# Modulation products beside the projections: issued in groups of eight and of four row blocks instead of two

## The chip, the cores and the metric

The kernel runs on one core of one Trainium2 chip. The core has TensorE (matrix products, 128 x 128 cells), VectorE, ScalarE, GpSimd and SyncE, which here only issues transfers; each works through its own list of instructions in order, and semaphores hold an instruction back until what it needs is there. The metric is the device time of one execution in microseconds (us), lower is better. Before the change it is 2209.9 us, the median of three runs (2208.8 to 2213.77).

## The reference

One step of a two-layer trunk over 1024 latent and 256 context tokens of width 1024, in 32-bit floats. Cut to the parts that matter here:

```python
def _pre(x, cond, p):
    mod = (jax.nn.silu(cond) @ p['w_ada'] + p['b_ada'])[:, None, :]
    shift, scale, gate = jnp.split(mod, 3, axis=-1)
    h = rms_norm(x, p['norm_g']) * (1 + scale) + shift
    parts = jnp.split(h @ p['w_in'], idx, axis=-1)
    return parts, gate

def _post(x, o_ret, o_gqa, o_mla, z_gate, g_res, w_out):
    y = jnp.concatenate([o_ret, o_gqa, o_mla], axis=-1) * jax.nn.silu(z_gate)
    return x + g_res * (y @ w_out)
```

`cond` is one vector for the latent tokens and one for the context tokens, so the modulation is a product of two rows of 1024 with a matrix `w_ada` of 1024 x 3072 in each layer: shift, scale and gate are its thirds. Between `_pre` and `_post` stand a retention, a grouped-query attention and a latent attention over the parts of `h @ w_in`.

## The kernel before

The tokens are ten tiles of 128. A projection block (`blk`, line 441) takes 256 columns of `w_in` (288 in one block) and makes, tile by tile, `act^T W` in one accumulator bank of PSUM (`project`, line 248). Activations and weights are each split into a high and a low part so that three fast products, lines 255 to 257, add up to full precision: 3 x 8 = 24 matmuls for a tile. The activations of the first layer are made while its first block runs (`phase_a`, line 373: transposes on TensorE, line 384, scale and shift on ScalarE and VectorE, lines 391 and 393, splits on ScalarE and VectorE, lines 401 and 402). The weights come as granules of two row blocks, are split by GpSimd (lines 191 and 192) and go into rings; three staging buffers, loaded at line 225, feed the splits, and a load into one of them waits until the split that read it last is done.

The modulation is `ada` (line 285). `cond` holds both conditioning vectors, 32 columns wide with two in use, so a product of one row block of 128 rows needs only 32 of the array's 128 columns. Four products can therefore stand side by side in four column tiles of the array (`tile_position`, line 329): row block k goes to column tile k % 4, and the tiles' sums are added afterwards. For each group of 256 columns, eight row blocks are multiplied, a load (line 316, 256 KB) bringing two of them at a time:

```python
for g in range(4):
    raw = raws.pop(0)
    for kk in range(2):
        k = 2 * g + kk
        ...
    load()
    yield
```

The `yield` is how this work is spread: `ada` is a generator, and each step of it runs after a tile of a projection block. The first two thirds of layer 0's modulation run ahead of everything. Its gate (columns 2048 to 3071, 64 products into tag "o", `gate_ada`, line 1463) runs beside the first projection block of layer 0, two steps after each tile. All of layer 1's modulation (96 products into tag "acc", `rest_of_ada`, line 1467) runs beside blocks two to seven of layer 0, one step after each tile and none in the fourth. Weights of the gate have a ring of eleven tiles, those of layer 1 a ring of three, of which `load()` fills at most two ahead. When a group of 256 columns is done, its sum is copied out (line 336) and, steps later, transposed (line 295).

The tag "acc" has five banks: four are free for projections while the modulation holds one. The tag "o" has a bank of its own.

What sets the order: the program is written in order, and a scheduler then places each engine's instructions by their dependences and priorities into the fixed list that the engine works through. SyncE issues nearly all transfers, also those of `w_in` and the stores of results, from one such list, so a transfer that waits holds back those after it.

Of the kernel before, what the change touches and what calls it, by code (L numbers as in the profile page):

```python
# [84 lines left out]
def hybrid_trunk(tc, I, O):  # L85
# [9 lines left out]
    # ------------------------------------------------------------------ DRAM scratch  # L95
# [12 lines left out]
    # ------------------------------------------------------------------ persistent pools  # L108
# [11 lines left out]
    def yh(t):  # L120
        """The columns of the attention heads, [P, GQA or MLA, head, 64]: head i of both side by side."""
        return yx[t][:, Y_H:].rearrange("p (i s c) -> p s i c", s=2, c=64)
# [21 lines left out]
    def newton(ss, n, c, bufs=4):  # L144
        """rsqrt(ss * c + EPS) for [P, n]."""
        x = sm.tile([P, 8], F32, name="nwx", tag="nwx")[:, :n]
        y = sm.tile([P, 8], F32, name="nwy", tag="nwy")[:, :n]
        u = sm.tile([P, 8], F32, name="nwu", tag="nwu")[:, :n]
        V.tensor_scalar(x, ss, c, EPS, op0=ALU.mult, op1=ALU.add)
        V.tensor_scalar(u.bitcast(I32), x.bitcast(I32), 1, None, op0=ALU.arith_shift_right)  # L150
        V.tensor_scalar(y.bitcast(I32), u.bitcast(I32), -1.0, float(0x5F3759DF), op0=ALU.mult, op1=ALU.add)
        V.tensor_scalar(x, x, -0.5, None, op0=ALU.mult)
        for _ in range(3):
            if n == 1:
                V.scalar_tensor_tensor(u, y, y, x, op0=ALU.mult, op1=ALU.mult)
            else:
                V.tensor_tensor(u, y, y, op=ALU.mult)
                V.tensor_tensor(u, u, x, op=ALU.mult)
            V.scalar_tensor_tensor(y, u, 1.5, y, op0=ALU.add, op1=ALU.mult)
        return y  # L160

    def rsq(ss, n, c):
        """rsqrt(ss * c + EPS) for [P, n]: exp(-ln / 2) and a Newton step."""
        return rsq_end(rsq_start(ss, n, c))
# [39 lines left out]
    class Weights:  # L204
        """Column blocks of [1024, *] matrices, split, as rings of K-granules of two row blocks."""
# [42 lines left out]
    def project(act, gran, n):  # L248
        """acc[tok, n] = act^T W, all three products of the split operands."""
        ps = bank("acc")[:, :n]  # L250
        ah, al = act
        for k in range(KC):
            wh, wl = gran[k // 2]
            wh, wl = wh[:, k % 2, :n], wl[:, k % 2, :n]
            T.matmul(ps, ah[:, k, :], wh, start=(k == 0), stop=False)  # L255
            T.matmul(ps, ah[:, k, :], wl, start=False, stop=False)  # L256
            T.matmul(ps, al[:, k, :], wh, start=False, stop=(k == KC - 1))  # L257
        return ps

    # ------------------------------------------------------------------ conditioning  # L260
# [12 lines left out]
    def ada_rows():  # L273
        """b_ada and norm_g of every layer with the columns on the partitions."""
        rows = wp.tile([P, 128], F32, name="brow", tag="msb", bufs=1)
        for l in range(DEPTH):
            dma(rows[32 * l:32 * l + 24, :], I["b_ada"][l].rearrange("(k p) -> k p", p=P))
            dma(rows[32 * l + 24:32 * l + 32, :], I["norm_g"][l].rearrange("(k p) -> k p", p=P))
        ps = bank("m")
        T.transpose(ps[:, :32 * DEPTH], rows[0:32 * DEPTH, :], ident[0:32 * DEPTH, 0:32 * DEPTH])  # L280
        for l in range(DEPTH):
            V.tensor_copy(biasT[l], ps[:, 32 * l:32 * l + 24])
            V.tensor_copy(normT[l], ps[:, 32 * l + 24:32 * l + 32])

    def ada(l, ns, pool, bufs, tag, wait=1, lag=1, done=None):
        """modT[l][:, 2n..2n+1, :] for the 256-column groups ns of the modulation; both
        conditionings at once, the row blocks of w_ada in four column tiles of the array."""
# [34 lines left out]
        for x, n in enumerate(ns):  # L322
            ps = bank(tag)[:, :256]
            for g in range(4):
                raw = raws.pop(0)
                for kk in range(2):
                    k = 2 * g + kk
                    j = k % 4
                    T.matmul(ps[32 * j:32 * j + 32, :], cond[:, k, :],
                             raw[:, kk, :], start=(k < 4), stop=(k >= 4), tile_position=(0, 32 * j))  # L330
                load()
# [20 lines left out]
    # ------------------------------------------------------------------ phase A: modulated norm, transposed and split  # L352
# [16 lines left out]
    def norm_x(t, junk):  # L369
        """x / rms(x) in place."""  # L370
        scale_x(t, rstd_x(t, junk))
# [32 lines left out]
    # ------------------------------------------------------------------ rope on natural [P, heads, dim]  # L404
    def rope(dst, src, cos, sin, h, dim, pa, eng=None):
        """dst = src * cos + rotate(src) * sin (signs are in sin)."""
# [13 lines left out]
    # ------------------------------------------------------------------ phase B: input projection  # L420
# [17 lines left out]
    def phase_b(l, p1, acts, ws, first, first_side, first_done, att):  # L438
# [63 lines left out]
        # ---- MLA query up-projection weights  # L502
# [16 lines left out]
        def cq_rest(t):  # L519
            """What is left of the tiles before t: transposes, up-projection, transposes, a tile per stage."""  # L520
# [38 lines left out]
        def cq_queries(t, qo):  # L559
            """The rotary queries of tile t transposed, to memory."""  # L560
# [42 lines left out]
        def headnorm(ps):  # L603
            """Per-head rms norm of four heads of 64."""
# [10 lines left out]
        def weighted_rope(g, nm):  # L615
            """rope tables with the norm weights in them: rope(x * g) = x * gc + rotate(x) * gs."""
# [38 lines left out]
        def gqa_transposed(t, o):  # L655
            """The queries of both attentions of tile t transposed in their place, the keys to memory."""
# [11 lines left out]
        def z_blk(c, post):  # L668
            """Gates of 256 columns with the columns on the partitions: the retention's, or those of two heads of each attention."""
# [64 lines left out]
    # ------------------------------------------------------------------ retention  # L734
# [12 lines left out]
    def decays(tmp):  # L747
        """log sigmoid of the decay logits (log1p as an atanh series), and the decays of every layer."""
# [16 lines left out]
        # q fwd, q bwd, k fwd, k bwd (the key scale 1/8 is in the last two)  # L765
# [7 lines left out]
    def retention(l, rt):  # L773
        if True:
# [20 lines left out]
            def increments(t, kv):  # L795
# [11 lines left out]
                # forward state after chunk t  # L807
# [4 lines left out]
                # backward increments, scanned below  # L812
# [87 lines left out]
    def cache_keys(l, pool, bufs):  # L900
        """The cached keys of both attentions, transposed."""
# [19 lines left out]
    def latents(l, lt):  # L921
        """Keys and values of the MLA heads from the compressed ones, in blocks of four chunks."""
# [56 lines left out]
    def decay_masks(l, pool, bufs):  # L979
        """The two directions' decays between the tokens of a chunk, with the key scale 1/8."""  # L980
# [23 lines left out]
    # ------------------------------------------------------------------ attention  # L1004
    class Attention:
# [3 lines left out]
        def prepare(self):  # L1009
            """Keys, values and queries of the first head, on the right side."""  # L1010
# [11 lines left out]
    def attention(l, att):  # L1022
        """Twelve heads over (latent pair x 4, context pair), software-pipelined by key banks:
        scores, softmax, transposes, values each some steps behind the one before."""
# [5 lines left out]
        # What keys and values are made of: pairs of a load into a staging tile and of its use  # L1030
# [9 lines left out]
        def k_items(i, src, K, split):  # L1040
            """[hi; lo] of 64 rows of transposed keys."""
# [57 lines left out]
        def kr_items():  # L1099
            """[hi; lo; hi; lo] of the transposed rotary keys, for rotary queries [hi; hi; lo; lo]."""  # L1100
# [16 lines left out]
        def q_piece(p):  # L1117
            """Queries of two token tiles, [hi; hi] and [lo; lo], and the rotary ones [hi; hi; lo; lo]."""
# [32 lines left out]
        def items():  # L1151
            """Keys and values of all heads, in the order of use; a function holds the uses after it back while it is false."""
# [14 lines left out]
        def step(force=False):  # L1167
            """Load an item, and use the one loaded some steps before."""
# [29 lines left out]
        # ---- the pipeline  # L1198
# [88 lines left out]
        def head_cols(p):  # L1287
            """Head p.i of both attentions, transposed, of two token tiles."""
# [4 lines left out]
        def y_job(p):  # L1293
            """The outputs of a pair of both heads by the sums of their softmaxes."""
# [11 lines left out]
        def advance(jobs):  # L1306
            """One pipeline step; jobs: the score job of this step, or none at the end."""
# [23 lines left out]
        # ---- pairs of token tiles: those of the GQA heads first, then in turn with those of the MLA heads  # L1331
# [63 lines left out]
    # ------------------------------------------------------------------ phase D: gate, output projection, residual  # L1395
# [5 lines left out]
    def phase_d(l, p1, acts, ws, after):  # L1401
        with tc.tile_pool(name=f"pg{l}", reuse_waits="tile", bufs=1, side="right") as pg, tc.tile_pool(name=f"pd{l}", reuse_waits="tile", bufs=1, side="right") as pd:
# [10 lines left out]
            def gated(t):  # L1413
                """The gated outputs of tile t, split; x comes back in their place."""
# [40 lines left out]
    # ------------------------------------------------------------------ the trunk  # L1455
# [7 lines left out]
    def gate_ada(pool, bufs):  # L1463
        yield from ada(0, range(8, 12), pool, bufs, "o", WG)
        ada_gate(0)

    def rest_of_ada(pool, bufs):
        yield from ada(1, range(12), pool, bufs, "acc", WR)
# [71 lines left out]
    for l in range(DEPTH):  # L1540
# [8 lines left out]
        def scale_late(t):  # L1549
            """1 / rms of tile t, and x / rms of the tile before it, whose copy is in s_x by then."""  # L1550
# [97 lines left out]
```

## Time and profile before

| | |
|---|---|
| median of three runs | 2209.9 us (2208.8 to 2213.77) |
| profiled execution: span from first to last instruction | 2203.2 us |
| distance of the median of the runs to that span | 6.7 us |
| TensorE busy | 2115.8 us, 96% |
| VectorE, ScalarE, GpSimd busy | 1555.0, 1183.4, 893.2 us |
| mean granted clock of TensorE | 0.990 of 2.4 GHz |

The profile is of one execution, and the other runs have no span of their own, so the 6.7 us stand for all that lies around the span. A matmul's row shows a start and a duration; matmuls are pipelined, so the step from one start to the next, not the duration, is what one costs in a stream. A row that ends in xN stands for N neighbouring instructions alike. A 32-bit product of `ada` leaves two records (two passes), and four of them make a pair. Text in brackets at a row's end is idle time of the engine before it and what ended it.

### The profile page before, as it was taken

What the parts mean: (1) busy time and instruction counts of PE and PEld (TensorE: products, weight loads), DVE (VectorE), ACT (ScalarE), POOL (GpSimd) and SP (SyncE); (2) the same over time, 40 slices, a digit from 0 to 9 for tenths busy, and PEclk for the clock granted to TensorE, in tenths of its full rate; (3) what the DMA queues carried; (4) which work ended last, traced back from release to release, by engine and by line L of the source; (5) the groups of instructions that cost most, each with busy time, mean ns of one, the idle gap of its engine ahead of it and who ended that gap; (6) DMA issues with size and microseconds to landing.
All of it is one profiled execution on the core that took longest, in us unless ns stands there. A gap on an engine that the chain in (4) does not pass through costs nothing. (4 is left out here: it accounts for less than half of the span.)

```text
span 2203.2 us, 42098 instructions
## 1 busy us (share of the span) xinstructions
PE 2115.8 (96%) x14928; PEld 1881.0 (85%) x14928; DVE 1555.0 (71%) x3987; ACT 1183.4 (54%) x3151; POOL 893.2 (41%) x1322
## 2 busy tenths in 40 slices
PE   7999999998999999999999999999899999999998
PEld 3789887877888888888999999888788888888898
DVE  4625474567898999998265357556699899999834
ACT  4503223233888888885244133313388888888623
POOL 2332232303756555432533314321375655443274
PEclk9999999999999999999999999999999999999999
DMA  9442435523100000014333212452310000001432
GB/s 322 126 137 60 122 93 167 159 64 100 32 25 20 22 21 16 5 51 124 97 133 108 59 51 58 130 158 75 95 42 23 22 23 22 11 9 32 135 101 96
DMA packets 196954, 173.15 MB, mean 79 GB/s; under 512 B 34968, under 2 KB 179208, under 8 KB 196744
## 3 DMA queue, kind: packets, MB, share of 16 engines
q1 hardware_dynamic: 195304, 165.21, 25.5%
q10 hardware_dynamic: 1440, 5.24, 0.6%
q8 instruction: 119, 1.95, 0.4%
q14 instruction: 91, 0.75, 0.1%
HBM read 124.64 MB, written 45.76 MB: 77 GB/s over the span
## 5 line engine op out<-in xcount | busy, mean ns | idle before, releaser
L257 PE MATMUL acc<-wh,al 128*128 128x256 f32 (+1 forms) x1760 | 500.0, 284 | 7.5 <-DVE al L402 7.4
L255 PE MATMUL acc<-wh,ah 128*128 128x256 f32 (+1 forms) x1760 | 505.3, 287 | 0.2
L256 PE MATMUL acc<-wl,ah 128*128 128x256 f32 (+1 forms) x1760 | 502.2, 285 | 0.0
L1219 DVE TENSOR_REDUCE nm<-acc 128x1 f32<-128x512 f32 (+1 forms) x624 | 412.2, 666 | 41.8 <-PE acc L1213 25.8
L1256 DVE TENSOR_TENSOR pT<-tp,pT 128x512 fp32r<-128x512 f32 (+1 forms) x624 | 413.2, 664 | 32.6 <-ACT pT L1255 27.4
L1255 ACT CAST pT<-tp 128x512 fp32r<-128x512 f32 (+1 forms) x624 | 356.1, 572 | 145.5 <-PE tp L1251 139.2
L1233 ACT ACTIVATE pn<-acc,nm 128x512 f32<-128x512 f32 (+1 forms) x624 | 421.4, 681 | 21.7 <-DVE nm L1224 19.6
L1251 PE MATMUL tp<-ident,pn 128*128 128x128 f32 x2400 | 424.7, 274 | 4.5 <-DVE pT L1256 3.0
L255 PEld LDWEIGHTS acc<-wh,ah 128*128 128x128 f32 x1760 | 334.3, 190 | 23.3 <-issue 9.1
L257 PEld LDWEIGHTS acc<-wh,al 128*128 128x128 f32 x1760 | 331.4, 188 | 11.1 <-DVE al L402 11.0
L256 PEld LDWEIGHTS acc<-wl,ah 128*128 128x128 f32 x1760 | 333.4, 189 | 1.2 <-issue 0.8
L1267 PE MATMUL o<-pT,V 128*128 128x256 f32 x1200 | 325.7, 293 | 0.8 <-DVE yx L1280 0.7
L1251 PEld LDWEIGHTS tp<-ident,pn 128*128 128x128 f32 x2400 | 288.5, 141 | 35.9 <-PE tp L1251 5.8
L1268 PE MATMUL o<-pT,V 128*128 128x256 f32 x1200 | 314.6, 284 | 0.0
L1267 PEld LDWEIGHTS o<-pT,V 128*128 128x128 f32 x1200 | 226.4, 189 | 19.8 <-DVE yx L1280 5.7
L1268 PEld LDWEIGHTS o<-pT,V 128*128 128x128 f32 x1200 | 226.7, 189 | 16.3
L191 POOL TENSOR_SCALAR wh<-raw 128x512 fp32r<-128x512 f32 (+2 forms) x144 | 84.8, 598 | 383.6 <-PE acc L257 150.1
L192 POOL TENSOR_TENSOR wl<-raw,wh 128x512 fp32r<-128x512 f32 (+2 forms) x144 | 166.5, 1167 | 4.9
L680 PE MATMUL acc<-ah,wh 128*128 128x512 f32 (+1 forms) x384 | 142.7, 372 | 0.0
L1210 PE MATMUL acc<-K,Qm 128*128 128x512 f32 (+1 forms) x312 | 140.5, 450 | 1.0
L681 PE MATMUL acc<-ah,wl 128*128 128x512 f32 (+1 forms) x384 | 139.4, 363 | 0.0
L682 PE MATMUL acc<-al,wh 128*128 128x512 f32 (+1 forms) x384 | 139.3, 363 | 0.0
(276 smaller groups left out, 3913.3 us busy)
## 6 DMA issues: line engine op xcount, KB each, us to landing
raw<-in_w_ada_dram SPq DMA_DIRECT2D x96, 256.0 KB, 3.5
raw<-in_w_in_dram SPq DMA_DIRECT2D x56, 256.0 KB, 3.7
s_gT<-eo SPq DMA_DIRECT2D x80, 128.0 KB, 2.5
kv<-s_rkv SPq DMA_DIRECT2D x40, 256.0 KB, 2.9
gt<-s_gT SPq DMA_DIRECT2D x20, 512.0 KB, 4.9
yx<-in_x_sample_dram SPq DMA_DIRECT2D x16, 512.0 KB, 8.6
raw<-in_w_in_dram SPq DMA_DIRECT2D x56, 128.0 KB, 2.2
raw<-in_w_out_dram SPq DMA_DIRECT2D x48, 128.0 KB, 3.0
```

Source lines behind the costliest of these rows:

```text
L192: G.tensor_tensor(wl, raw, wh.bitcast(F32), op=ALU.subtract)
L255: T.matmul(ps, ah[:, k, :], wh, start=(k == 0), stop=False)
L256: T.matmul(ps, ah[:, k, :], wl, start=False, stop=False)
L257: T.matmul(ps, al[:, k, :], wh, start=False, stop=(k == KC - 1))
L680: T.matmul(ps, wh, ah[:, k, :], start=(k == 0), stop=False)
L1219: V.tensor_reduce(nm[:, b:b + 1], ps, axis=AX.X, op=ALU.max, negate=True)
L1233: A.activation(pn, ps, AF.Exp, bias=p.ng[i], accum_out=p.su[:, i, b:b + 1])
L1251: T.transpose(pt[:, c * 128:(c + 1) * 128], pn[:, c * 128:(c + 1) * 128], ident)
L1255: A.copy(ph, p3)
L1256: V.tensor_tensor(pl, p3, ph.bitcast(F32), op=ALU.subtract)
L1267: T.matmul(p.po, vc, p.gran[b][:, 0, c, :], start=(ch == 0), stop=False)
L1268: T.matmul(p.po, vc, p.gran[b][:, 1, c, :], start=False, stop=(ch == last))
```

## The change

`ada` gets a parameter `group`, and the products of `group` steps are issued together in the last of them; the steps before it issue nothing, and `load()` is called only after a group. The steps and their number are as before. `group` is 4 (eight row blocks, all of a column group) for the gate of layer 0, 2 (four row blocks) for layer 1, and 1, the old order, for the part of layer 0 ahead of the projections. Comments are taken out, too; lines behind `ada`'s head move down by one or two.

```diff
-    def ada(l, ns, pool, bufs, tag, wait=1, lag=1, done=None):
+    def ada(l, ns, pool, bufs, tag, wait=1, lag=1, done=None, group=1):
...
             for g in range(4):
-                raw = raws.pop(0)
-                for kk in range(2):
-                    k = 2 * g + kk
-                    j = k % 4
-                    T.matmul(ps[32 * j:32 * j + 32, :], cond[:, k, :],
-                             raw[:, kk, :], start=(k < 4), stop=(k >= 4), tile_position=(0, 32 * j))
-                load()
+                if g % group == group - 1:
+                    for k in range(2 * (g + 1 - group), 2 * (g + 1)):
+                        raw, j = raws[0], k % 4
+                        T.matmul(ps[32 * j:32 * j + 32, :], cond[:, k, :],
+                                 raw[:, k % 2, :], start=(k < 4), stop=(k >= 4), tile_position=(0, 32 * j))
+                        if k % 2:
+                            raws.pop(0)
+                    load()
                 yield
...
     def gate_ada(pool, bufs):
-        yield from ada(0, range(8, 12), pool, bufs, "o", WG)
+        yield from ada(0, range(8, 12), pool, bufs, "o", WG, group=4)
         ada_gate(0)
 
     def rest_of_ada(pool, bufs):
-        yield from ada(1, range(12), pool, bufs, "acc", WR)
+        yield from ada(1, range(12), pool, bufs, "acc", WR, group=2)
         ada_gate(1)
```

Three places of the engines' lists show what moves. The first is TensorE in the first projection block, at the gate's first group; `raw` is the modulation's weights, `yx` a token tile being transposed, and line 384 of before is line 386 of after. Before:

```order
L256 MATMUL acc<-wl,ah_122 128x256
L257 MATMUL acc<-wh,al_123 128x256
L329 MATMUL o<-raw,cond 32x256 x2
L384 MATMUL tp<-ident,yx 128x128 x3
L329 MATMUL o<-raw,cond 32x256 x2
L384 MATMUL tp<-ident,yx 128x128 x5
```

and after:

```order
L256 MATMUL acc<-wl,ah_122 128x256
L257 MATMUL acc<-wh,al_123 128x256
L329 MATMUL o<-raw,cond 32x256 x6
L386 MATMUL tp<-ident,yx 128x128 x3
L329 MATMUL o<-raw,cond 32x256 x2
L386 MATMUL tp<-ident,yx 128x128 x5
```

The group's eight products were four runs of two, the last two of which are shown; they have become one run of six and one of two, and the projection's matmuls that parted the first runs stand ahead of them all. The rest of the gate is in runs of 8, then 1, 1 and 6, and 8, where there were twelve runs of 2.

The second is TensorE in the second projection block, at layer 1's modulation; the rows are the projection's matmuls with a run of products between two tiles. Before:

```order
L257 MATMUL acc<-wh,al_125 128x256
L329 MATMUL acc<-raw,cond 32x256 x2
L255 MATMUL acc<-wh,ah_124 128x256
L256 MATMUL acc<-wl,ah_124 128x256
L257 MATMUL acc<-wh,al_125 128x256
```

and after:

```order
L257 MATMUL acc<-wh,al_125 128x256
L329 MATMUL acc<-raw,cond 32x256 x4
L255 MATMUL acc<-wh,ah_124 128x256
L256 MATMUL acc<-wl,ah_124 128x256
L257 MATMUL acc<-wh,al_125 128x256
```

A run has four products and not two, and comes after each second tile. Over the whole of layer 1 there are 49 runs before and 25 after; one group of four is parted by a transpose, where two pairs were.

The third is SyncE between the second and the third projection block; `raw` from `w_ada` is a load of the modulation, from `w_in` one of the projections' weights, two parts to a granule here, and `raw_1628` is the same tenth load of layer 1 in both. Line 316 of before is line 317 of after. Before:

```order
L225 DMA raw_2006<-in_w_in_dram 128x2x128
L492 DMA s_rkv0_60<-eo_1577 128x256
L316 DMA raw_1628<-in_w_ada_dram 128x2x256
L225 DMA raw_2006<-in_w_in_dram 128x2x160
L225 DMA raw_2130<-in_w_in_dram 128x2x128
L225 DMA raw_2130<-in_w_in_dram 128x2x160
L225 DMA raw_2299<-in_w_in_dram 128x2x128
L316 DMA raw_1665<-in_w_ada_dram 128x2x256
```

and after:

```order
L225 DMA raw_2002<-in_w_in_dram 128x2x128
L494 DMA s_rkv0_60<-eo_1577 128x256
L225 DMA raw_2002<-in_w_in_dram 128x2x160
L225 DMA raw_2126<-in_w_in_dram 128x2x128
L225 DMA raw_2126<-in_w_in_dram 128x2x160
L225 DMA raw_2295<-in_w_in_dram 128x2x128
L225 DMA raw_2295<-in_w_in_dram 128x2x160
L317 DMA raw_1628<-in_w_ada_dram 128x2x256
```

The tenth load stood between the parts of the projection's granules and stands behind all of them now.

## Rows read from the trace of the kernel before

**Rows 1.** Section 1 of the page: busy time, share, instructions
```profile
PE 2115.8 (96%) x14928; PEld 1881.0 (85%) x14928; DVE 1555.0 (71%) x3987; ACT 1183.4 (54%) x3151; POOL 893.2 (41%) x1322
```

**Rows 2.** Busy time by stretch; columns in the first row
```profile
core 0: us, PE busy (x) PEld busy (x) DVE busy (x) ACT busy (x) POOL busy (x), PEclk, DMA share, GB/s
57.00:93.00 36.00, 35.74 (x274) 26.84 (x273) 25.76 (x59) 27.32 (x71) 6.86 (x6) 1.00 0.35 106
109.00:168.00 59.00, 58.87 (x459) 49.63 (x460) 12.92 (x47) 2.24 (x6) 23.27 (x28) 1.00 0.47 136
221.00:341.00 120.00, 120.00 (x914) 101.78 (x914) 75.04 (x304) 35.92 (x138) 37.01 (x57) 1.00 0.37 105
```

**Rows 3.** Waits of TensorE, 50 to 345 us: total, times, longest
```profile
PE acc L329 <- DMA raw<-in_w_ada_dram: 0.6, 1, 0.6
...
PE o L329 <- DVE part L336: 0.3, 1, 0.3
PE acc L257 <- DVE al L402: 0.2, 1, 0.2
```

**Rows 4.** Timeline of TensorE around a pair: start, duration, row
```profile
134.26 0.28 PE L257 MATMUL acc<-wh,al 128*128 128x256 f32 x1
134.47 0.63 PE L329 MATMUL acc<-raw,cond 128*32 128x256 f32 x4
135.03 0.39 PE L255 MATMUL acc<-wh,ah 128*128 128x256 f32 x1
135.25 0.28 PE L256 MATMUL acc<-wl,ah 128*128 128x256 f32 x1
```

**Rows 5.** Timeline: four products in a row, and three in the tail
```profile
33.37 0.16 PEld L329 LDWEIGHTS acc<-raw,cond 128*32 128x32 f32 x8 [0.17 <-issue]
33.38 0.64 PE L329 MATMUL acc<-raw,cond 128*32 128x256 f32 x8
...
340.10 0.63 PE L329 MATMUL acc<-raw,cond 128*32 128x256 f32 x6
340.66 0.50 PE L680 MATMUL acc<-ah,wh 128*128 128x512 f32 x1
```

**Rows 6.** Records of tile cond, 33.4 to 34 us: durations, first and last start
```profile
L329 PE MATMUL acc<-raw,cond x8: 379/391/403, 33.4 to 33.6; 128*32 128x256 f32 x8
```

**Rows 7.** The same view from 50 to 345 us: counts
```profile
L329 PE MATMUL acc<-raw,cond x192: 376/379/403, 109.1 to 340.4; 128*32 128x256 f32 x192
...
L329 PE MATMUL o<-raw,cond x64: 379/391/403, 57.1 to 92.5; 128*32 128x256 f32 x64
```

**Rows 8.** Waits of VectorE and ScalarE, 50 to 94 us
```profile
DVE axv L393 <- ACT axv L391: 4.2, 8, 1.3
DVE al L402 <- ACT ah L401: 3.0, 7, 0.8
...
ACT axv L391 <- PE tp L384: 5.8, 6, 1.7
```

**Rows 9.** Loads of w_ada from 94 us on: issue to landing
```profile
DMA to landing us min/median/max: 2.8/3.0/4.3
```

**Rows 10.** Timeline of SyncE and TensorE, second and third projection block
```profile
114.32 0.37 SPq L225 DMA_DIRECT2D raw<-in_w_in_dram  x1
...
119.89 0.63 PE L329 MATMUL acc<-raw,cond 128*32 128x256 f32 x4
...
134.12 0.37 SPq L316 DMA_DIRECT2D raw<-in_w_ada_dram  x1
...
138.02 0.51 SPq L316 DMA_DIRECT2D raw<-in_w_ada_dram  x1
138.58 0.46 SPq L225 DMA_DIRECT2D raw<-in_w_in_dram  x1
...
141.67 0.63 PE L329 MATMUL acc<-raw,cond 128*32 128x256 f32 x4
```

**Rows 11.** Waits of SyncE, 104 to 345 us
```profile
SPq L225 <- POOL wl L192: 26.8, 17, 3.3
```

## Prediction, made before the changed kernel ran

> **What bounds the kernel now.** I read section 1 of the page first, then the table of stretches, then the waits of TensorE, then single rows. Section 1 has TensorE busy for 2115.8 us of a span of 2203.2 [rows 1]. A share over the whole span says nothing of the stretches that the change touches, so the next view is the busy time by stretch [rows 2]: from 57 to 93 us (first projection block of layer 0 with its gate products) TensorE works 35.74 of 36 us, from 109 to 168 us (second and third block, with layer 1's modulation) 58.87 of 59, and from 221 to 341 us (fifth to seventh block) 120.00 of 120, all at granted clock 1.00, the 2.4 GHz level. The reader is to see that there is no idle TensorE time to win there, and that time taken off TensorE's list is time off the span unless something else is late. What else could be late is in the waits: over the 295 us from 50 to 345 TensorE waited for a load of modulation weights 0.6 us, for a copied partial sum 0.3 us, for an activation split 0.2 us [rows 3]. VectorE and ScalarE have room in the later stretch (75.04 and 35.92 of 120 us) and little in the first (25.76 and 27.32 of 36) [rows 2].
>
> **What a pair costs.** In the steady part of the second block [rows 4] a projection matmul starts each 0.12 us. Around a pair of modulation products (one "x4" row: each product is two records) the starts are 134.26, pair at 134.47, next projection matmul at 135.03, the one after at 135.25. That is 0.99 us from the last matmul before to the second after it; two ordinary steps are 0.24; so the pair costs 0.99 - 0.24 = 0.75 us. Most of it is not work in proportion to the products: the pair starts 0.09 late, the next matmul starts 0.56 after the pair, and the following one is another 0.10 late. This change of shape of the array, from full width to four tiles of 32 columns and back, is what is paid per run and not per product.
>
> **What four in a row cost.** The start phase of the same kernel has runs of four products whose weights had all come: one "x8" row lasts 0.64 us against 0.63 for a pair, with all eight weight loads inside 0.16 us [rows 5]. A run of three products in the seventh block's tail is followed by a projection matmul 340.66 - 340.10 = 0.56 us after it, the same distance as behind a pair. And in the x8 row the first records start at 33.4 and the last at 33.6: four products go through their two passes side by side [rows 6]. So four products in four different column tiles cost what two cost, plus some 0.02 us of weight loads.
>
> The Trainium skill has a rule against this: "TensorE: Matmul & The Clock Gate", part 3, The mechanism, says that a weight load overlaps running matmuls only when its row group differs. The four column tiles here share all rows, so by it the second pair's loads would wait and a run of four would last like two pairs' streams, which is the second rival below. The x8 row with its eight loads inside 0.16 us does not agree with it as far as different column tiles go.
>
> **Layer 1, groups of four.** Its 96 products are 192 records from 109.1 to 340.1 us [rows 7], 48 pairs. The order on TensorE has them in 49 runs before (two pairs lie around a transpose) and 25 after (one group does). 24 runs fewer by 0.75 us is 18.0; 24 fuller runs by 0.02 is 0.5 back: 17.5 us gained. Bounds of the term: 18.0 if the loads hide; at the low end, the second half of each group streams alone. From one pass to the next is 0.2 us [rows 6], two passes 0.43, so the gain would be 24 x (0.75 - 0.43) = 7.7.
>
> **Layer 0's gate, groups of eight.** 64 records from 57.1 to 92.3 us [rows 7] are 16 pairs, 16 x 0.75 = 12.0 us. The new order has seven runs: 6 and 2 products, 8, then 1, 1 and 6, and 8. Eight products are two rounds over the four column tiles, so four of these runs have a second round on tiles that are in use. No row shows one with its weights at hand. Its price is between two passes, 0.43, and a whole further run, 0.75; I take 0.5, near the passes, since no change of shape lies between. 7 x 0.75 + 4 x 0.5 = 7.25; TensorE's list gets 12.0 - 7.25 = 4.75 us shorter (3.75 to 5.0). Not all of it reaches the span: here the activations are normalized, modulated and split while the block runs. VectorE idles 4.2 and 3.0 us for ScalarE, so the two are chained, and ScalarE waits for TensorE's transposes 5.8 us in 44 [rows 8]. That 5.8 us is the slack from which 4.75 would come, nearly all of it. I take 70%, 3.3 us; ends 0 and 5.0. What is late next, if it is used up, is the split of the activations (line 402), for which TensorE waits 0.2 us now.
>
> **Loads of the weights.** A group of four consumes two 256 KB tiles of a ring of three. In the changed order the second tile of a group can be asked for only when the group before has let go of its first, two blocks (some 5.7 us) ahead of use, where a single pair had three blocks. A load lands 2.8 to 4.3 us after its issue, median 3.0 [rows 9], so 2.7 us are left for what stands ahead of it in SyncE's queue. At one place that is not enough. Load raw_1628 (the tenth) stood at 134.12 us [rows 10] between the projection's loads; in the new order it stands behind all of them, which wait for GpSimd's splits. The last of them is issued at 138.58 for 0.46 us, so ends at 139.04; less the two modulation loads that no longer stand between (0.4 and 0.5), and less the 2.85 us by which everything is earlier by then (six pairs gone, three groups there, 3 x 0.75, and the 0.6 us wait of the first pair, which now comes a block later), raw_1628 goes out at 135.3 and lands at 138.3 to 138.5. Its group would start at 141.67 - 0.6 - 9 x 0.75 + 4 x 0.77 = 137.4 [rows 10]. A new wait of 1.1 us (0 to 2.4 with the landing's spread). Two others are level within some tenths: the second group's last load behind the projection load of 114.32, landing near 117.7 for a start at 119.89 - 0.6 - 1.5 = 117.8, and a load behind the like train near 303 us; 0.4 us for both. Queued behind a waiting group are the next block's projection matmuls, so such a wait is paid in full. The first pair's 0.6 us goes. Net 0.9 us lost (0.6 gained to 4 lost).
>
> **What costs nothing.** VectorE does the same work in the stretch from 221 to 341 us, shortened by some 9 us: 75.04 of 111, still under 70%; if its chain were late, four accumulators ahead cover it, and beyond that its lag would be TensorE's. The copies of the partial sums and their transposes are as many as before. The loads are as many.
>
> **Sum.** 17.5 + 3.3 - 0.9 = 19.9 us off the span of 2203.2, so 2183.3. The median of the runs, 2209.9, lies 6.7 above the profiled span; I leave that distance alone: 2190.0 us. What follows the projections runs in the same order and only starts earlier.
>
> **Rivals.** First, the gate's gain is lost wholly to the chain of ScalarE and VectorE, and the late loads cost their 4 us: 17.5 - 4 = 13.5, 2196. For it: ScalarE is busy 27.32 of 36 us there and would be at 87% of 31 us. Against it: TensorE waits 0.2 us now.
>
> Second, products beyond the first two run one after the other, as if only the tiles already loaded went side by side: 7.7 + 2 (the gate, whose later rounds would each cost 0.43 more) - 0.9, some 9 us, 2201. The run of four stands against it [rows 5, 6].
>
> Third, on the other side: the loads become the bound for every group. Place: SyncE's queue ahead of the second load of each group. For it: SyncE waits 26.8 us in 17 places for GpSimd's splits, the longest 3.3 [rows 11]. Each group has 2.7 us in hand. It decides when the mean wait of 23 groups passes (17.5 + 3.3 + 4.4) / 23 = 1.1 us, a delay of 3.8 us at every group; with 1.3 us each it is 30 us lost, 2203.2 - 20.8 + 30 + 6.7 = 2219. Against it: only three of 23 places have a waiting train ahead in the new order.
>
> Fourth, the runs cost per product after all (the pair's 0.75 is just two products): no change, 2210. The rows of the runs of three and four contradict it [rows 5].
>
> **How the numbers follow.** Forecast 0.74, first rival 0.13, second 0.07, third 0.03, fourth 0.03. A change of 0.2% (4.4 us) is about the least that a measurement of this kernel can tell. The first three cases are faster by more: 0.94; within: 0.03; slower: 0.03. The forecast's own ends: the loads hidden and the gate whole give 18 + 5 + 0.6 = 23.6, 2186; the first rival gives 2196. With a microsecond for the runs' own spread, 2185 to 2198; outside lie the second and later rivals.
>
> **What would show it.** In the changed profile: "x8" rows for layer 1 lasting about 0.65 us with a projection matmul 0.56 after their start, 24 of them; a "x16" row of the gate some 1.05 to 1.15 us long; the end of the seventh block some 20 us earlier than 341; a wait of about 1 us of a group for a load near 137 us; waits of TensorE for line 402 below 2 us. Wrong would be: x8 rows of 1 us and more (second rival), waits for modulation weights at most groups (third), or line 402 waiting 4 us and more before 93 us (first).

## The result, and the profile after

The changed kernel takes 2184.6 us (median of four runs, 2183.5 to 2185.9) where the kernel before took 2209.4 on the same chip (four runs, 2208.5 to 2213.8): 24.7 us less by these medians. The ratio on record is 0.9897 with a 95% interval of 0.9882 to 0.9911, 20 to 26 us less; it is not the ratio of the two medians, which is 0.9888. The forecast of 2190.0 had the sign and the mechanism; the median lies 0.4 us below the low end of its range, while the ratio, taken from the 2209.9 that the forecast started from, gives 2187.1, inside it.

Section 1 of the page of the changed kernel, to be read against [rows 1]:

```profile
span 2184.1 us, 42090 instructions
...
PE 2099.5 (96%) x14928; PEld 1882.1 (86%) x14928; DVE 1553.7 (71%) x3987; ACT 1181.4 (54%) x3151; POOL 890.7 (41%) x1322
```

The instructions counted here are as many as before on every engine. TensorE has 16.3 busy us less and the span is 19.1 shorter. The same work got shorter by standing in another order.

The table of stretches, columns as in [rows 2]:

```profile
57.00:93.00 36.00, 35.58 (x306) 30.21 (x305) 24.93 (x59) 27.50 (x72) 8.08 (x8) 1.00 0.38 116
109.00:168.00 59.00, 58.48 (x496) 53.85 (x497) 14.92 (x52) 4.34 (x15) 28.11 (x32) 1.00 0.48 141
221.00:321.00 100.00, 100.00 (x845) 90.71 (x844) 70.48 (x277) 33.04 (x125) 34.90 (x56) 1.00 0.41 120
```

TensorE is as full as it was, at the same granted clock of 1.00 (the 2.4 GHz level), but more matmuls pass in the same time: 306 in the 36 us of the first stretch where 274 passed, 496 in 59 us where 459 did.

The next rows are the timeline of TensorE (start, duration, row) at five places: a whole group of the gate, an early group of layer 1, one whose second half waits, one in mid-course, and the last group, which a transpose parts:

```profile
88.60 0.28 PE L257 MATMUL acc<-wh,al 128*128 128x256 f32 x1
88.81 1.07 PE L329 MATMUL o<-raw,cond 128*32 128x256 f32 x16
89.81 0.39 PE L255 MATMUL acc<-wh,ah 128*128 128x256 f32 x1
...
114.58 0.28 PE L257 MATMUL acc<-wh,al 128*128 128x256 f32 x1
114.79 1.09 PE L329 MATMUL acc<-raw,cond 128*32 128x256 f32 x8
115.81 0.38 PE L255 MATMUL acc<-wh,ah 128*128 128x256 f32 x1
...
134.84 0.63 PE L329 MATMUL acc<-raw,cond 128*32 128x256 f32 x4
135.99 0.62 PE L329 MATMUL acc<-raw,cond 128*32 128x256 f32 x4 [0.52 <-DMA raw<-in_w_ada_dram]
136.54 0.39 PE L255 MATMUL acc<-wh,ah 128*128 128x256 f32 x1
...
221.09 0.64 PE L329 MATMUL acc<-raw,cond 128*32 128x256 f32 x8
221.66 0.40 PE L255 MATMUL acc<-wh,ah 128*128 128x288 f32 x1
...
319.11 0.62 PE L329 MATMUL acc<-raw,cond 128*32 128x256 f32 x2
319.66 0.44 PE L296 MATMUL tp<-ident,part 128*128 128x128 f32 x2
320.03 0.63 PE L329 MATMUL acc<-raw,cond 128*32 128x256 f32 x6
320.59 0.50 PE L682 MATMUL acc<-ah,wh 128*128 128x512 f32 x1
```

An x8 row with its weights there lasts 0.64 us and the projection goes on 221.66 - 221.09 = 0.57 after its start; 21 of layer 1's groups look like that. A pair had 0.56 [rows 4]: the second pair of a group costs 0.01. In the gate's x16 row, two rounds over the four column tiles, the next matmul follows 1.00 after the start, so the second round costs 1.00 - 0.56 = 0.44. The x8 row at 114.79 is 0.45 longer than its like. The group at 134.84 has the next matmul 136.54 - 134.84 = 1.70 after its start, where 0.57 is usual: 1.13 lost, of which the row in brackets shows 0.52 as idle. These are the two late loads, 1.58 in all; the third place that was feared, near 303 us before, shows none. In a second profile of the changed kernel the late group near 134 is there again (1.22 lost), and the one near 114 is whole: its load is late in some executions only. The run of three products that stood at 340.10 [rows 5] stands at 320.03.

The waits of TensorE from 50 to 345 us (total, times, longest) answer to [rows 3]:

```profile
PE tp L914 <- DMA raw<-in_cache_gqa_k_dram: 0.9, 1, 0.9
PE acc L329 <- DMA raw<-in_w_ada_dram: 0.5, 1, 0.5
...
PE acc L257 <- DVE al L404: 0.4, 1, 0.4
```

Line 404 is line 402 of before: the split of the activations holds TensorE for 0.4 us in one place and not for the 4 that would have spoken for the first rival. All late steps of the first block together, those shorter than this view counts with them and not all for that split, are 1.4 us when read one by one in the timeline, where the kernel before has 0.2. Two rows of the kernel before belong beside these, the first from 345 to 420 us, the second from 50 to 345:

```profile
PE tp L912 <- DMA raw<-in_cache_gqa_k_dram: 1.1, 1, 1.1
...
PE tp L533 <- DVE e L515: 0.5, 1, 0.5
```

The first says that the wait of line 914, for a load of cached keys behind the projections, is not new: the kernel before has it at its line 912, some 20 us later and outside the window of [rows 3]. The second, a transpose of the fourth block that waits for VectorE, is gone in the changed kernel. It is also gone with layer 1 alone changed and is there with the gate alone changed; why stays open.

To see where the gain arises I follow one matmul, line 257, to three landmarks: the first of the third tile of the first block, the first of the second block, and the first of the ninth tile of the seventh block. In the kernel before:

```profile
55.31 0.39 PE L257 MATMUL acc<-wh,al 128*128 128x256 f32 x1 [0.18 <-DVE al L402]
...
96.20 0.28 PE L257 MATMUL acc<-wh,al 128*128 128x256 f32 x1
...
331.34 0.28 PE L257 MATMUL acc<-wh,al 128*128 128x256 f32 x1
```

and in the changed one:

```profile
56.18 0.28 PE L257 MATMUL acc<-wh,al 128*128 128x256 f32 x1
...
93.21 0.28 PE L257 MATMUL acc<-wh,al 128*128 128x256 f32 x1
...
311.26 0.28 PE L257 MATMUL acc<-wh,al 128*128 128x256 f32 x1
```

The gate's stretch went from 40.89 to 37.03 us, a gain of 3.86, and layer 1's from 235.14 to 218.05, a gain of 17.09. Together 20.95; the changed execution was 0.87 late at the first landmark, ahead of the change, and took 1.0 longer from the third landmark to its end, which leaves the 19.1 us of the span. The same distances in the other profiles (us; the first row whole, the others against it, minus is shorter), and what lies behind the third landmark up to the span's end, whole:

| kernel | gate's stretch | layer 1's stretch | behind the third landmark |
|---|---|---|---|
| before | 40.89 | 235.14 | 1872 |
| before, second profile | +0.04 | +0.01 | 1871 |
| changed | -3.86 | -17.09 | 1873 |
| changed, second profile | -3.59 | -17.47 | 1871 |
| gate alone changed | -3.63 | -0.19 | 1871 |
| layer 1 alone changed | +0.06 | -16.85 | 1880 |
| both, two column tiles per group in layer 1 | -3.69 | -9.52 | 1880 |
| both, layer 1's loads on ScalarE's queue | -3.58 | -18.29 | 1876 |
| both, gate in groups of four | -3.07 | -17.90 | 1871 |
| layer 1 as changed, gate full width in pairs | +4.06 | -16.62 | 1876 |

The two stretches repeat within 0.4 us from one profile of a kernel to the next. What lies behind them differs by 10 us between executions, without order by kernel, although nothing but layer 1's last runs of products was changed there. So the stretches carry the argument, and a difference of a few microseconds between times does not.

### The profile page after: what moved, and what is told of

It is laid out like the page before. It is cut to its first block, busy times and chain, and to the rows that moved or that the text cites. A ratio compares the mean times of both kernels' runs of the same rounds, so it can differ in the third digit from the quotient of the medians.

```text
span 2184.1 us, 42090 instructions
## 1 busy us (share of the span) xinstructions
PE 2099.5 (96%) x14928; PEld 1882.1 (86%) x14928; DVE 1553.7 (71%) x3987; ACT 1181.4 (54%) x3151; POOL 890.7 (41%) x1322
## 5 line engine op out<-in xcount | busy, mean ns | idle before, releaser
L1270 PEld LDWEIGHTS o<-pT,V 128*128 128x128 f32 x1200 | 227.1, 189 | 16.3
L1134 POOL TENSOR_SCALAR Qm<-yx 64x256 fp32r<-64x256 f32 x120 | 48.2, 402 | 223.9 <-PE acc L1213 217.2
```

The lines of the kernel that those rows point to most:

```text
L1270: T.matmul(p.po, vc, p.gran[b][:, 1, c, :], start=False, stop=(ch == last))
```

## The experiments

**The gate alone.** The call of layer 1 goes back to pairs; against the changed kernel:

```diff
     def rest_of_ada(pool, bufs):
-        yield from ada(1, range(12), pool, bufs, "acc", WR, group=2)
+        yield from ada(1, range(12), pool, bufs, "acc", WR)
```

> Only layer 0's gate in groups of eight row blocks; layer 1 in pairs as before. Theory (a run of products costs 0.31 us for the change of the array's shape and 0.44 us for each round over the four column tiles): 16 runs of one round become 7 runs with 11 rounds, 12.0 - 7.0 = 5.0 us off TensorE's list, of which 3.9 to 5 reach the time: 2204.5 to 2205.5 us against 2209.4 of before. Rival (ScalarE and VectorE pace this block, the gain seen in the changed kernel at 93 us is chance): 2208 to 2210 and the block's end within 1 us of before.

Measured: 2203.0 us (11 runs) against 2206.8 of before (23 runs), ratio 0.9981 (0.9972 to 0.9989), 3.8 us less, just under the 3.9 to 5 expected. Its stretch in the trace is 3.63 shorter, and the lead stays at 3.8 to the third landmark. The gate's gain reaches the span. The first rival, that ScalarE and VectorE's chain eats it, falls: TensorE waits 0.7 us in two places for line 404.

**Layer 1 alone.** The mirror of it:

```diff
     def gate_ada(pool, bufs):
-        yield from ada(0, range(8, 12), pool, bufs, "o", WG, group=4)
+        yield from ada(0, range(8, 12), pool, bufs, "o", WG)
```

> Only layer 1 in groups of four; layer 0's gate in pairs as before. Theory: 49 runs become 25, 24 x 0.75 = 18, less some 1.5 us of waits for late loads, plus 0.6 us of a wait that goes: 17 us less than before, 2192.5 us. The two gains add up to that of the whole change. Rival (something else than the runs gives part of the 24.7 us between the medians, such as the order of transfers): this kernel and the gate alone add up to 21 us and leave 3 to 4 us that neither has, or one of the two has it in a stretch without products.

Measured: 2191.9 us (6 runs), ratio 0.9929 (0.991 to 0.9947), 12 to 20 us less. The trace has nothing in the gate's stretch (+0.06) and 16.85 in layer 1's. The two halves' 3.63 + 16.85 = 20.5 are the 20.95 of both within half a microsecond, so they add up in the trace and neither needs the other. By the medians of the runs, 3.8 and 14.9, they leave 3.4 of the 22.1 us by which the changed kernel lies below the same 2206.8. These six runs go from 2185.1 to 2196.6, and the profiled one is over 9 us longer than the changed kernel's second profile behind the third landmark, so the medians can't say more.

**The kernel before, once more.** The kernel before, unchanged, for what a run's time is made of.

> The kernel before, run and profiled again. The time of the changed kernel's runs lies 1.8 us above their spans, while the profiled span of before, 2203.2, lay 6.2 us under the median of its runs. If that one execution was simply a quick one, spans of 2205 to 2209 are seen here, each 1.8 us under its time, and the time is 2209.4. If the distance is the kernel's own, spans near 2203 with times near 2209 are seen.

Measured: 2205.4 us (12 runs, 2202.5 to 2212.4), ratio 0.9996 (0.9984 to 1.0008). Each run has a time and a span, and they are 1.8 us apart in the quickest and in the slowest: 2202.52 and 2200.7, 2212.36 and 2210.6. So the profiled execution of before, span 2203.2, took about 2205.0 us: a quick one of its kernel, and not one with 6.7 us around it.

**The same column tiles twice.** Layer 1's groups of four use two column tiles, two products on each, in place of four; the accumulation flags move with them, so that the sum stays whole:

```diff
-                        raw, j = raws[0], k % 4
+                        raw, j = raws[0], 2 * (k // 4) + k % 2 if l else k % 4
                         T.matmul(ps[32 * j:32 * j + 32, :], cond[:, k, :],
-                                 raw[:, k % 2, :], start=(k < 4), stop=(k >= 4), tile_position=(0, 32 * j))
+                                 raw[:, k % 2, :], start=(k % 4 < 2 if l else k < 4), stop=(k % 4 >= 2 if l else k >= 4), tile_position=(0, 32 * j))
```

> The changed kernel, but layer 1's groups of four use two column tiles twice (0, 1, 0, 1, then 2, 3, 2, 3) in place of four tiles once. Runs and their number as in the changed kernel. Theory (price by rounds): 24 groups have a second round, 24 x 0.44 = 10.6 us slower than the changed kernel, 2195 us; rows of a group 1.07 us long in place of 0.64. Rival (what is saved is the number of runs alone, products are free in any tiles): 2184.6 us as the changed kernel. Rival (loads of weights wait for running products also in the changed kernel, so that the tiles make no difference): 2184.6 us too, with rows of equal length in both.

Measured: 2194.8 us (6 runs), ratio 0.9947 (0.993 to 0.9964), some 10 us over the changed kernel. TensorE's timeline in it:

```profile
115.40 1.06 PE L329 MATMUL acc<-raw,cond 128*32 128x256 f32 x8
116.39 0.39 PE L255 MATMUL acc<-wh,ah 128*128 128x256 f32 x1
```

Its weight loads, and those of a like group of the changed kernel:

```profile
122.30 0.58 PEld L329 LDWEIGHTS acc<-raw,cond 128*32 128x32 f32 x8
```

```profile
221.09 0.16 PEld L329 LDWEIGHTS acc<-raw,cond 128*32 128x32 f32 x8 [0.20 <-issue]
```

Four products on two tiles cost 0.99 us and not 0.57, and their loads spread over 0.58 us in place of 0.16. That is 0.42 us for a second round, and the 22 groups ahead of the third landmark make 9.2. The stretch lost 17.09 - 9.52 = 7.6; its groups come later and meet no late load, which gives back the changed kernel's 1.58: 7.6 + 1.58 = 9.2, so all of it is seen. What makes four as cheap as two is that each has a column tile of its own.

**Layer 1's loads on ScalarE's queue.**

```diff
-                dma(raw, w[g * 256:(g + 1) * 256, n * 256:(n + 1) * 256].rearrange("(k p) c -> p k c", p=P))
+                (A.dma_start if l else dma)(raw, w[g * 256:(g + 1) * 256, n * 256:(n + 1) * 256].rearrange("(k p) c -> p k c", p=P))
```

> The changed kernel, with layer 1's modulation loads issued from ScalarE's queue in place of SyncE's. Theory (the two late groups, 0.45 us near 115 and 1.15 us near 135 in the changed kernel's trace, are loads held back in SyncE's list by loads of projection weights that wait for GpSimd): both waits go, the seventh block ends 1.6 us earlier than in the changed kernel, the time is 2183 us against 2184.6, which is less than the runs can tell, so the trace decides. Rival (the ring of three tiles leaves too little time for a landing, whoever issues it): both waits stay. Rival (ScalarE, which issues in order, is held by loads that wait for TensorE, and the projections wait for ScalarE's copies): new waits of TensorE, time above 2186.

Measured: 2186.0 us (4 runs), ratio 0.9894 (0.9878 to 0.9911): no difference in time from the changed kernel that can be told. In the trace the two groups that had waited:

```profile
115.11 0.64 PE L329 MATMUL acc<-raw,cond 128*32 128x256 f32 x8
115.68 0.38 PE L255 MATMUL acc<-wh,ah 128*128 128x256 f32 x1
...
134.71 0.64 PE L329 MATMUL acc<-raw,cond 128*32 128x256 f32 x8
135.28 0.39 PE L255 MATMUL acc<-wh,ah 128*128 128x256 f32 x1
```

Both are whole again. So the late loads were late in SyncE's list, behind loads that waited for GpSimd, and not in the memory: the same loads, asked for at the same depth of ring but from a list in which nothing waits ahead of them, come in time. The group near 134, layer 1's fifth, shows it: it waits in all the five profiles with groups of four over four column tiles whose loads go through SyncE, and not here. The one near 115 does not, since the second profile of the changed kernel has it whole, too. Layer 1's stretch gains 0.8 to 1.2 us by it (18.29 against 17.47 and 17.09).

**The gate in groups of four.** `group=2` in `gate_ada`; eleven runs in place of seven.

> The changed kernel, but layer 0's gate in groups of four row blocks in place of eight; TensorE's list then has 11 runs of one round each where it has 7 runs with 11 rounds. Theory (0.31 us a run, 0.44 a round): 4 runs more at 0.31 are 1.2 us more, so the gate's block ends 1.2 us later than in the changed kernel; time 2185.8. Rival (second rounds are as dear as runs, 0.75): 11 runs for 7 runs with 4 dear rounds, no difference.

Measured: 2186.9 us (4 runs), ratio 0.9901 (0.9885 to 0.9917). The stretch is 37.82 us, 0.5 and 0.8 longer than in the two profiles with groups of eight and not the 1.2 expected: row by row, TensorE's list is 1.2 longer, and its late steps in the block are some 0.5 shorter. The times can't tell the two apart. Most of the gate's gain is in the first doubling.

**The gate in full width.** Its products fill the array's 128 columns, without column tiles, in pairs, their conditioning padded with zeros; the rings of weights of layer 0, the gate's and that of the part ahead of the projections, have ten tiles, not eleven. Layer 1 stays as changed.

```diff
-        cond = pool.tile([P, KC, 32], F32, name="cond", bufs=1)
+        cond = pool.tile([P, KC, 128 if wide else 32], F32, name="cond" + "w" * wide, bufs=1)
...
+                        if wide:
+                            T.matmul(ps, cond[:, k, :], raw[:, k % 2, :], start=(k == 0), stop=(k == 7))
+                        else:
...
-        yield from ada(0, range(8, 12), pool, bufs, "o", WG, group=4)
+        yield from ada(0, range(8, 12), pool, bufs, "o", WG, wide=True)
```

> Layer 0's gate with the stationary side padded to 128 columns, so that the products use the whole width of the array and no column tiles; in pairs, as before, and layer 1 in groups of four. The ring of gate weights has ten tiles, not eleven. Theory (the 0.31 us of a run are paid for the change of the array's shape): a pair costs its two streams one after the other, 0.90, and hardly more, so 16 pairs are 16 x 0.2 = 3 us dearer than column-tiled pairs: the block's stretch from 55 us to the gate's end is 3 us longer than in the kernel with layer 1 alone in groups. Rival (the 0.31 us are paid for the change of the kind of product, 32-bit in two passes after fast ones): 0.90 + 0.31 for a pair, 16 x 0.46 = 7 us longer.

Measured in one run: 2197.4 us. TensorE's timeline at a pair:

```profile
66.87 0.28 PE L256 MATMUL acc<-wl,ah 128*128 128x256 f32 x1
66.99 0.28 PE L257 MATMUL acc<-wh,al 128*128 128x256 f32 x1
67.11 1.02 PE L330 MATMUL o<-raw,condw 128*128 128x256 f32 x4
67.97 0.38 PE L296 MATMUL tp<-ident,part 128*128 128x128 f32 x2
```

The pair starts 0.12 us after the matmul ahead of it, like any matmul of the stream, where a pair in column tiles starts 0.21 after it [rows 4]. It then takes 0.86, four passes of 0.215 one after the other. So nothing is paid ahead of it for a change of shape, and its own length is what two products cost. The stretch is 4.06 us longer than before; 1.1 of that is a wait of a transpose for VectorE's modulation, and in the other 3.0 the 16 pairs of 0.86 in place of 0.70 to 0.75 make 2.3, and three pairs that follow transposes cost 0.2 more each. The fixed part of a column-tiled run is the way there and back.

**The changed kernel, once more.**

> The changed kernel again, on the chip and beside the runs of before that the other kernels of this call have. Theory: the trace's gain up to the end of the seventh block, 20 us, is the whole gain, so the medians differ by 19 to 22 us, and the 24.7 us of the first comparison came from runs of before that were on the slow side of their spread (2202.5 to 2213.8). Rival: 24 to 25 us again, and 4 us of it come from somewhere behind the projections.

Measured: 2184.7 us (4 runs, 2181.9 to 2188.8) against 2208.7 (7 runs), ratio 0.9893 (0.9876 to 0.9911), span of the profile 2181.2. By medians that is 24 us, the rival's number; against the 23 runs of before in the first experiments it is 22.1, at the upper end of the theory's. All 46 runs of before and all eight of the changed kernel together have medians of 2207.1 and 2184.6, 22.5 apart. The spans of single profiles give 2203.2 - 2184.1 = 19.1 and 2203.2 - 2181.2 = 22.0, the landmarks 20.95 and 21.06. The runs of one kernel spread over 4 to 12 us, and the table shows that the profiles differ behind the third landmark, so the one or two us between the traces and the medians stay open. From 60 to 320 us the granted clock is 1.00 in every profile. Stretches at a lower one lie ahead of that (0.83 from 40 to 60 us in both kernels) and behind it (slices with 0.81 and 0.83 in before, 0.77 and 0.74 in the changed kernel); I did not tell their shares apart.

Groups of eight in layer 1, the obvious next step, were not tried: they need a ring of more than three weight tiles there, and whether the memory beside them has room for it no run shows.

## Why the prediction was right, and where it was not

**What a pair costs, and four in a row: right.** The pair's 0.75 us was split into a fixed part and a part per round. The runs now give the split: 0.44 us per round over the column tiles (x16 row; 0.42 in the experiment with two tiles), and 0.31 for going there and back, 0.09 ahead, 0.10 behind, and 0.12 left in between. The Trainium skill's "TensorEngine Tiling (Array Packing)", Key Properties, says that changing the tiling mode drains TensorE. The trace agrees as far as it can show: each change of mode and back has a fixed cost of 0.31 us beside projection matmuls, and the full-width pair, which changes no mode, has none. The Trainium skill's rule that was weighed against the change ("TensorE: Matmul & The Clock Gate", part 3, The mechanism: a weight load overlaps running matmuls only when its row group differs) does not agree with these traces for column tiles. With all rows shared, eight loads went in 0.16 us when each column tile had only the two of one product, and spread over 0.58 us when a second product's loads went to the same tile.

**Layer 1, 17.5 us: right.** 17.09 to the landmark, with the late loads in it. Put back the 1.58 that they cost, take off the 0.6 of the first pair's wait that went [rows 3] and the 0.5 of line 533's, which the forecast did not have: 17.09 + 1.58 - 0.6 - 0.5 = 17.6, against the 17.5 taken. The third landmark stands ahead of the last groups, but 24 runs fewer lie ahead of it, as in the whole.

**The gate, 4.75 us times 70%: right, with both terms of the list half a microsecond high.** The run price was taken as 0.75 for each, from a pair between projection matmuls; in the first block most pairs had transposes behind them. Such a pair in the timeline of the kernel before:

```profile
65.30 0.28 PE L257 MATMUL acc<-wh,al 128*128 128x256 f32 x1
65.51 0.62 PE L329 MATMUL o<-raw,cond 128*32 128x256 f32 x4
...
66.07 0.44 PE L295 MATMUL tp<-ident,part 128*128 128x128 f32 x2
66.44 0.62 PE L329 MATMUL o<-raw,cond 128*32 128x256 f32 x4
```

The start is 0.09 late and the transpose follows after 0.56. The two transposes take 0.37 up to the next pair, where two ordinary steps, 0.11 each, would be 0.22: 0.09 of the rest lies ahead of that pair, and 0.06 behind this one. So a pair before transposes costs 0.70. Eleven such pairs and five of 0.75 are 11.5, the seven new runs by the same reckoning 6.7, with second rounds of 0.44 and not 0.5: 4.8 us of list, and 0.3 more for a wait on a partial sum that went [rows 3]. Of those 5.1 the stretch got 3.6 to 3.9, 70 to 75%; the late steps of the block, 1.4 us against 0.2, are the rest. The forecast of 3.3 is short by the 0.3 of the wait and little more. That 12.0 and 7.25 were high by the same half microsecond is luck; the 70% was a guess that came out.

**Loads of the weights: right in place and size.** Forecast were 1.1 us for the tenth load's group near 137 us and 0.4 for two marginal places; the trace has 1.13 at 134.84, 0.45 at 114.79 and nothing at the third (in the profile of layer 1 alone 0.28 there). The group comes 2.6 us earlier than the forecast's 137.4, since the gate's gain was left out of that sum. That it was the queue was argued then, and is shown for the first of them by the loads on ScalarE's list.

**The sum of the span: 2183.3 against 2184.1, and 2181.2 in the second profile.** The saving of 19.9 is 1.1 short of the 21.0 to the landmarks. That what follows the projections "only starts earlier" holds no closer than executions repeat there: the two took 1873 and 1871 us, the kernel before 1872 and 1871.

**The distance of 6.7 us and the runs' spread: mis-sized.** "I leave that distance alone" is the same as taking 19.9 off the median of three runs, 2209.9. The distance is not one thing that lies around the span: that is 1.8 us, and the other 4.9 were how far apart a profiled execution and three other runs happened to be, of a kernel whose runs spread from 2202.5 to 2213.8. 23 more runs of before had their median at 2206.8, twelve others at 2205.4 and seven at 2208.7; over all 46 it is 2207.1, so the starting point was some 3 us high, and from there the same saving gives 2187.2. Of the 5.4 us by which the forecast was too high, 2.8 are that. Of the other 2.6, 1.1 is the saving to the landmarks (21.0, not 19.9), and 1.5 stays open, within what these runs can say. The step that failed is "a microsecond for the runs' own spread": it should have been three or four, and the range, which the median leaves by 0.4 us, would have reached lower by that.

**The rivals.** The first (gate lost to the chain, 4 us of late loads) falls by the gate alone, 3.8 us. The second (products beyond two one after the other) falls by the x8 rows, and the experiment with two tiles shows what it would have looked like in layer 1: rows of 1.06 us and 2194.8, where the rival, with the gate's part in it, had 2201. The third (a wait at each group) falls: two groups of 24 wait, and in the second profile one. The fourth (cost per product) falls with the rows and the result.

## What to carry to other kernels

Where small products stand between large ones in another shape of the array, price the excursion and the round apart, from one short and one long run in the trace: here 0.31 and 0.44 us, so filling all column tiles of an excursion is worth more than any later doubling. Grouping work means asking for its data in groups as well: look in the issuing queue for what waits ahead of each group's last load, and price those places one by one. Where the runs of a kernel spread, a median of three is itself uncertain by some microseconds, and the range of a forecast has to hold that beside the mechanism.

## What was not expected of the hardware

An excursion with transposes behind it costs 0.05 us less than one between projection matmuls: the late step behind it is 0.06 and not 0.10. A pair in full width costs 0.86 us and one in column tiles 0.75, so the column tiles save a pair only 0.1 us; it is four products that they make cheap. The time of a run is its span plus 1.7 to 1.9 us in every run that had both. And the runs of one program on one core spread over 10 us in 23 runs (2202.75 at mean granted clock 0.990, 2212.64 at 0.985), over two and a half times the 3.8 us of the gate's change: that half could be told from nothing only by many runs, or by the landmarks in the trace.
